# Two fp32 transformer blocks on one core: 64-row band scores issued in pairs, and 16 meta keys padded to 128 rows

## The chip, the core and the metric

The kernel runs on one core of a Trainium2 chip. A core has five engines with a queue each: TensorE (PE; its weight loads are listed apart as PEld), VectorE (DVE), ScalarE (ACT), GpSimd (POOL) and SyncE (SP), which here only issues DMA transfers. TensorE reads SBUF and writes PSUM; VectorE and ScalarE carry results from PSUM to SBUF. The metric is the device time of one execution in microseconds (us), lower is better.

## The reference, cut to what matters

Two blocks run one after the other over 256 tokens of width 2048, all in fp32. The first mixes by a gated scan over eight heads and by an attention over bands of chunks with 16 heads of width 64, then has an MLP of width 8192. The second puts 16 meta tokens in front, has two attentions (A: eight query heads of width 128 on two key heads; B: eight heads, each with two score maps of width 64 and one value of width 128), and keeps only the 256 real tokens. The two attentions that the change touches:

```python
# first block, band attention: 16 heads of width 64
s = jnp.einsum('bhnqd,bhnkd->bhnqk', qc, kb) * (Dh ** -0.5) + bias[:, None]
p = jax.nn.softmax(jnp.where(valid[:, None, :], s, -jnp.inf), axis=-1)
o = jnp.einsum('bhnqk,bhnkd->bhnqd', p, vb)
# second block, mixer A; 272 keys, 16 of them meta tokens
s = jnp.einsum('bkgqd,bksd->bkgqs', qs[0], k) * scale
o = jnp.einsum('bkgqs,bksd->bkgqd', jax.nn.softmax(s, axis=-1), v)
# second block, mixer B
a = jax.nn.softmax(s1, axis=-1) - lam * jax.nn.softmax(s2, axis=-1)
o = jnp.einsum('bhqk,bhkd->bhqd', a, v)
```

## The kernel before, in words

The linear layers are one long stream. `run_stream` (from line 223) walks over all weights in pieces of 1 MB, which SP loads into three buffers (line 240). Each piece is worked in two halves. ScalarE rounds a half to a high part `wh` (line 256, three halves ahead), VectorE makes the low part `wl` (line 268, two halves ahead), and TensorE multiplies both by the operand, which is split in the same way: three fp32r matmuls per tile of 128x128, twelve to a half with 512 columns (line 307), or, in those layers of the second block whose result is wanted transposed, 24 with 272 columns (line 305).

Everything else is a side task, written as a Python generator. `gap` runs at the middle and at the end of a half and advances the tasks of `bg` and `post` by one step, so a task's instructions stand in every engine's queue behind the half in which the step was taken. The order is fixed when the program is built; nothing is scheduled at run time. The queues are in order, and tiles come from pools: ten SBUF tiles `w2`, four PSUM banks `ps`. An instruction that takes a tile over waits until its last reader is done.

`band(c)` (line 544) handles eight heads, and runs twice. In an even step `j` it issues the scores of head `j // 2`: two matmuls over 64 rows (width 64), one of 128 and one of 256 columns (lines 584, 585), with even heads on partitions 0 to 63 and odd heads on 64 to 127; then a fused add and maximum for each (lines 589, 591), a scale and two exponentials (lines 594, 595). In odd steps an earlier head's probabilities are transposed (line 602), copied (line 604), and one step pair later multiplied by the values (lines 613 to 615).

`att_a` (line 925) and `att_b` (line 993) do the second block's mixers, each twice, in eight units of one head and 128 queries. The 272 keys are two blocks of 128 and one of 16 meta keys. `probs_T` transposes the three blocks; the third has 16 columns as weights (line 985). `probs_out` copies them out of PSUM with two instructions (lines 989, 990). The value product adds three matmuls, of which the third has 16 rows (line 970 in A, line 1051 in B). `ev2_nat` (line 809) brings the values into natural order, with those of the meta tokens in a tile of 16 partitions. The scores of B (line 1028) are two matmuls over 64 rows, one on each half of the partitions, issued back to back.

An fp32 matmul (not fp32r) runs as two passes, each a weight load and a matmul in the trace.

Of the kernel before, what the change touches and what calls it, by code (L numbers as in the profile page):

```python
# [27 lines left out]
def two_blocks_kernel(  # L28
# [85 lines left out]
    def split(dst, k0, n, src, scale=None):  # L114
        """dst[:, :, k0:k0+n] <- hi and lo of src [P, n, 256] (times a column per kt)."""
        if scale is None or not isinstance(scale, (list, tuple)):
            hi, lo = dst[:, 0, k0:k0 + n, 0:256], dst[:, 1, k0:k0 + n, 0:256]
            if scale is None:
                act(out=hi, in_=src, func=AF.Copy)
                tt_(out=lo, in0=src, in1=hi.bitcast(F32), op=ALU.subtract)  # L120
            else:
                act(out=hi, in_=src, func=AF.Copy, scale=scale)
                stt(out=lo, in0=src, scalar=scale, in1=hi.bitcast(F32), op0=ALU.mult, op1=ALU.subtract)
            return
        for k in range(n):
            hi, lo = dst[:, 0, k0 + k, 0:256], dst[:, 1, k0 + k, 0:256]
            act(out=hi, in_=src[:, k], func=AF.Copy, scale=scale[k])
            stt(out=lo, in0=src[:, k], scalar=scale[k], in1=hi.bitcast(F32), op0=ALU.mult, op1=ALU.subtract)

    def xpose_split(src, name, g, colscale=None, one=None):  # L130
        """generator: the group g of operand `name` from src [token, 2, 512] natural."""
        dst = op_tile(name, g)
        if name == "z":
            mt = mt_t[0][:, 4 * g:4 * g + 4, :]
            act(out=dst[:, 0, :, 256:NKEY], in_=mt, func=AF.Copy)
            tt_(out=dst[:, 1, :, 256:NKEY], in0=mt, in1=dst[:, 0, :, 256:NKEY].bitcast(F32), op=ALU.subtract)
        for half in range(2):
            p = ps([P, 2, 256])
            for k in range(2):
                for t in range(2):  # L140
                    c = (half * 2 + k) * P
                    nc.tensor.transpose(p[:, k, t * P:(t + 1) * P], src[:, t, c:c + P], ident_)  # L142
            if colscale is not None:
                sc = [colt[:, colscale + 4 * g + 2 * half + k:colscale + 4 * g + 2 * half + k + 1] for k in range(2)]
            else:
                sc = one
            split(dst, 2 * half, 2, p, sc)
            if half == 0:
                yield True
        ops[name, g] = dst  # L150
        yield True

# [53 lines left out]
    class Job:  # L206
        """One block of columns of a layer: 512 with the tokens stationary, or (`keys`) 256 with
        the weights stationary, which leaves the result transposed, the meta tokens behind the others."""
# [125 lines left out]
    def start(issue, prepare):  # L334
# [27 lines left out]
        def rest():  # L362
# [18 lines left out]
            # lower bounds: softmax over the two rows, its first row  # L381
# [162 lines left out]
    def band(c):  # L544
# [29 lines left out]
        for j in range(16 + 4):  # L574
            if j == 5:
                load_bias(1)
            if j % 2 == 0 and j < 16:
                h = j // 2
                pr, e = h // 2, (h % 2) * 64
                if h % 4 == 0:  # L580
                    st[h // 4] = sm([P, 2, 4])
                p = ps([P, 384])
                q0, k0 = qT[e:e + 64, pr], kT[e:e + 64, pr]
                nc.tensor.matmul(p[:, 0:P], lhsT=q0[:, 0:P], rhs=k0[:, 0:P], start=True, stop=True)  # L584
                nc.tensor.matmul(p[:, P:384], lhsT=q0[:, P:256], rhs=k0, start=True, stop=True)  # L585
                s = w2([P, 384])
                mx = sm([P, 4])
                tb = tbs[h // 4][:, h % 4]
                nc.vector.tensor_tensor_reduce(out=s[:, 0:P], in0=p[:, 0:P], in1=tb[:, P:256], scale=1.0, scalar=-3.0e38,
                                               op0=ALU.add, op1=ALU.max, accum_out=mx[:, 0:1])  # L590
                nc.vector.tensor_tensor_reduce(out=s[:, P:384], in0=p[:, P:384], in1=tb, scale=1.0, scalar=-3.0e38,
                                               op0=ALU.add, op1=ALU.max, accum_out=mx[:, 1:2])
                ts_(out=mx[:, 2:4], in0=mx[:, 0:2], scalar1=-1.0, scalar2=None, op0=ALU.mult)
                act(out=s[:, 0:P], in_=s[:, 0:P], func=AF.Exp, bias=mx[:, 2:3], accum_out=st[h // 4][:, 0, h % 4:h % 4 + 1])
                act(out=s[:, P:384], in_=s[:, P:384], func=AF.Exp, bias=mx[:, 3:4], accum_out=st[h // 4][:, 1, h % 4:h % 4 + 1])
                sT[h] = s
# [199 lines left out]
    def ev2_keysT(c, sub):  # L796
        """two heads of transposed keys of the second mixer"""
        def f(accs):
            ensure("rbc")
            if sub == 0:  # L800
                nat["kb", c] = c4([P, 4, NKEY])
            for k in range(2):
                tt_(out=nat["kb", c][:, 2 * sub + k], in0=accs[k], in1=rbc, op=ALU.mult)
            if sub == 1:
                flags.add(("kb", c))
                bg.append(att_b(c))
        return f

    def ev2_nat(key, sub, meta_shape, then=None):
        """256 columns with the tokens back on the partitions, the meta tokens apart"""  # L810
# [6 lines left out]
        def back(t):  # L817
            for _ in range(2):
                yield False
            if sub == 0:  # L820
                nat[key] = c4([P, 2, NCH]), w2(meta_shape)
            v, m = nat[key]
# [13 lines left out]
            act(out=m2[:, cs], in_=p, func=AF.Copy, scale=st2[0:META, 0:1])  # L836
# [7 lines left out]
    def rope(v, nh, qk, t):  # L844
        """v [P, nh, 128] in place, with the gain."""
# [10 lines left out]
    def head_norm(v, nh, dst, parts=P):  # L856
        """dst [parts, nh] <- rsqrt of the mean square of each head of v."""
# [8 lines left out]
    def keys_a():  # L866
# [9 lines left out]
        head_norm(vmA[:, 0], 2, rm, parts=META)  # L876
# [8 lines left out]
        for h in range(2):  # L885
            stt(out=vmA[:, 0, h], in0=vmA[:, 0, h], scalar=rm[:, h:h + 1], in1=qkg[0:META, 1], op0=ALU.mult, op1=ALU.mult)
# [3 lines left out]
        for h in range(2):  # L890
# [3 lines left out]
            nc.tensor.transpose(p[:, 256:NKEY], vmA[:, 0, h], ident[0:META, 0:META])  # L894
# [5 lines left out]
    def transposed(src, dst, scales=None):  # L900
        """dst [P, 4, >=256] <- the four blocks of src, transposed (times a constant each)."""
# [23 lines left out]
    def att_a(c):  # L925
# [18 lines left out]
        for j in range(16 + 4):  # L944
            if j % 2 == 0 and j < 16:
# [8 lines left out]
                s = w2([P, NKEY])  # L954
                act(out=s, in_=p, func=AF.Exp, bias=z[:, 0:1], scale=z[:, 1:2], accum_out=z[:, 2:3])
# [8 lines left out]
            if j % 2 == 1 and 0 <= u < 8:  # L964
# [5 lines left out]
                nc.tensor.matmul(p, lhsT=w[0:META, 2, :], rhs=vmA[:, 1, c], start=False, stop=True)  # L970
# [10 lines left out]

    def probs_T(s, p):
        nc.tensor.transpose(p[:, 0, :], s[:, 0:P], ident_)
        nc.tensor.transpose(p[:, 1, :], s[:, P:256], ident_)
        nc.tensor.transpose(p[0:META, 2, :], s[:, 256:NKEY], ident_)

    def probs_out(p):
        w = w2([P, 3, P])
        nc.vector.tensor_copy(out=w[:, 0:2], in_=p[:, 0:2])
        nc.vector.tensor_copy(out=w[0:META, 2], in_=p[0:META, 2])  # L990
        return w

    def att_b(c):
# [19 lines left out]
        for j in range(16 + 6):  # L1013
            if j % 2 == 1 and 0 <= (j - 3) // 2 < 8:
# [5 lines left out]
                stt(out=e[0], in0=e[1], scalar=z[:, 7:8], in1=e[0], op0=ALU.mult, op1=ALU.add)  # L1020
            if j % 2 == 0 and j < 16:
# [4 lines left out]
                for k in range(2):  # L1026
                    p = ps([P, NKEY])
                    nc.tensor.matmul(p, lhsT=qT[64 * k:64 * k + 64, h, t * P:(t + 1) * P], rhs=kT[64 * k:64 * k + 64, h],  # L1028
                                     start=True, stop=True)
                    s = w2([P, NKEY])  # L1030
                    nc.vector.tensor_tensor_reduce(out=s, in0=p, in1=dist[:, t], scale=1.0, scalar=-3.0e38,
# [3 lines left out]
                for k in range(2):  # L1035
                    act(out=e[k], in_=e[k], func=AF.Exp, bias=z[:, 2 + k:3 + k], scale=slope, accum_out=z[:, 4 + k:5 + k])
# [8 lines left out]
            if j % 2 == 1 and 0 <= u < 8:  # L1045
# [5 lines left out]
                nc.tensor.matmul(p, lhsT=w[0:META, 2, :], rhs=vmB[:, h // 2, h % 2], start=False, stop=True)  # L1051
# [88 lines left out]
    def proj_b(c):  # L1140
# [3 lines left out]
        for u in range(2):  # L1144
            J(w_in_2, 0, 4608 + NCH * c + 256 * u, "z", 4, ev2_nat(("vb", c), u, [META, 2, 2, P]), True)
# [5 lines left out]
    for u in range(2):  # L1151
        J(w_in_2, 0, 1024 + 256 * u, "z", 4, ev2_nat("kv", u, [META, 2, 2, P], lambda: bg.appendleft(keys_a())), True)
# [79 lines left out]
```

## Time and profile before

| | |
|---|---|
| three timed runs | 1972.69 us median (1971.82 to 1972.81) |
| span of the profiled execution | 1971.6 us; the page gives no other time of it, so what lies around the span is read as the median less the span, 1.1 us |
| TensorE matmuls | 1950.7 us busy, 99% |
| TensorE weight loads | 1597.3 us, 81%, beside the matmuls |
| VectorE, ScalarE, GpSimd | 1093.6 us (55%), 900.5 us (46%), 41.7 us (2%) |
| DMA | 344.88 MB, mean 175 GB/s |

A busy share says how long an engine had something in hand, not that it worked at its best. Matmuls are pipelined: the printed duration of one is longer than the time from its start to the next one's, so the cost of a group of matmuls is read from starts. A time in brackets behind a row is how long the engine sat idle before it, with what ended that.

### The profile page before, as it was taken

How to read it: one execution, taken by the hardware profiler on the slowest of the kernel's cores; microseconds unless marked ns; L12 is line 12 of the kernel's file. 1: busy time of each engine (PE TensorE's matmuls, PEld its weight loads, DVE VectorE, ACT ScalarE, POOL GpSimd, SP SyncE). 2: the span in 40 equal slices, each digit the busy share in tenths (PEclk: the TensorE clock that was granted, in tenths of full speed). 3: DMA queues.
4: the chain of work that ended last, by engine and by line, in shares of the span. 5: the costliest groups of instructions: out<-in, count | busy, mean ns of one | idle time of the engine just before them, and what ended most of it. 6: DMA issues, size and time to landing. Idle time of an engine off the chain costs nothing.

```text
span 1971.6 us, 23902 instructions
## 1 busy us (share of the span) xinstructions
PE 1950.7 (99%) x9438; PEld 1597.3 (81%) x9438; DVE 1093.6 (55%) x1555; ACT 900.5 (46%) x1267; POOL 41.7 (2%) x49
## 2 busy tenths in 40 slices
PE   8999999999999999999999999999999999999997
PEld 6888887878888888888888888888888998878886
DVE  5666655544446655554555555446566555566554
ACT  6344344454444445443444344335454444456442
POOL 0000010000000000000000000000000100000000
PEclk9999999999999999999999999999999999999999
DMA  8444464445555556555665555556555533434553
GB/s 307 150 150 169 152 202 142 168 150 169 185 185 184 185 181 191 180 191 184 186 199 183 185 187 171 196 189 211 172 188 175 171 129 129 150 129 150 171 182 117
DMA packets 183441, 344.88 MB, mean 175 GB/s; under 512 B 5840, under 2 KB 28368, under 8 KB 183328
## 3 DMA queue, kind: packets, MB, share of 16 engines
q1 hardware_dynamic: 181632, 337.70, 51.3%
q0 software_dynamic: 1696, 5.65, 0.9%
q8 instruction: 74, 1.21, 0.2%
q14 instruction: 39, 0.32, 0.0%
HBM read 341.23 MB, written 2.10 MB: 174 GB/s over the span
## 4 chain that ended last, share of the span: by engine, by line
PE 92%; issue 6%; DMA 1%; DVE 0%; SPq 0%; POOL 0%; POOLq 0%; DVEq 0%; ACT 0%; ACTq 0%
PE acc L307 78%; PE acc L305 6%; PE sp L142 1%; PE sp L456 1%; DMA raw<-in_w_in_dram 1%; PE sp L1028 1%; PE sp L585 0%; PE sp L949 0%; PE sp L584 0%; PE sp L1051 0%; PE sp L602 0%; PE sp L970 0%; DVE c L1091 0%; PE sp L478 0%; PE sp L1050 0%
## 5 line engine op out<-in xcount | busy, mean ns | idle before, releaser
L268 DVE TENSOR_TENSOR wl<-raw,wh 128x1024 fp32r<-128x1024 f32 (+1 forms) x634 | 770.9, 1218 | 449.8 <-PE acc L307 368.5
L256 ACT ACTIVATE wh<-raw 128x1024 fp32r<-128x1024 f32 (+1 forms) x634 | 667.6, 1055 | 656.3 <-PE acc L307 612.0
L307 PE MATMUL acc<-wh,op_u 128*128 128x512 f32 x1408 | 466.7, 401 | 8.2 <-ACT wh L256 6.7
L307 PE MATMUL acc<-wh,op_v 128*128 128x512 f32 x1024 | 327.0, 395 | 0.0
L307 PE MATMUL acc<-wh,op_h 128*128 128x512 f32 x1024 | 323.9, 394 | 0.0
L307 PEld LDWEIGHTS acc<-wh,op_u 128*128 128x128 f32 x1408 | 265.2, 188 | 71.9 <-ACT wh L256 6.7
L307 PE MATMUL acc<-wl,op_u 128*128 128x512 f32 x704 | 278.3, 395 | 1.0 <-DVE wl L268 1.0
L307 PEld LDWEIGHTS acc<-wh,op_h 128*128 128x128 f32 x1024 | 192.3, 188 | 44.0
L307 PEld LDWEIGHTS acc<-wh,op_v 128*128 128x128 f32 x1024 | 192.3, 188 | 43.5
L307 PE MATMUL acc<-wl,op_h 128*128 128x512 f32 x512 | 201.8, 394 | 0.0
L307 PE MATMUL acc<-wl,op_v 128*128 128x512 f32 x512 | 201.7, 394 | 0.0
L307 PE MATMUL acc<-wh,op_z 128*128 128x512 f32 x512 | 177.4, 407 | 0.0
L307 PEld LDWEIGHTS acc<-wl,op_u 128*128 128x128 f32 x704 | 132.9, 189 | 29.2 <-DVE wl L268 2.2
L305 PE MATMUL acc<-op_z,wh 128*128 128x272 f32 x640 | 130.1, 295 | 0.0
L307 PEld LDWEIGHTS acc<-wh,op_z 128*128 128x128 f32 x512 | 96.1, 188 | 27.6 <-issue 4.3
L307 PEld LDWEIGHTS acc<-wl,op_h 128*128 128x128 f32 x512 | 96.1, 188 | 22.3
L307 PEld LDWEIGHTS acc<-wl,op_v 128*128 128x128 f32 x512 | 96.1, 188 | 21.7
L305 PEld LDWEIGHTS acc<-op_z,wh 128*128 128x128 f32 x640 | 102.4, 188 | 2.5 <-issue 1.1
L307 PE MATMUL acc<-wl,op_z 128*128 128x512 f32 x256 | 100.8, 394 | 0.0
L305 PE MATMUL acc<-op_z,wl 128*128 128x272 f32 x320 | 92.1, 288 | 0.0
L307 PE MATMUL acc<-wh,op_mg 128*128 128x512 f32 x256 | 82.1, 396 | 0.0
L307 PE MATMUL acc<-wh,op_y 128*128 128x512 f32 x256 | 80.6, 394 | 0.0
(262 smaller groups left out, 1664.7 us busy)
## 6 DMA issues: line engine op xcount, KB each, us to landing
raw<-in_w_in_dram SPq DMA_DIRECT2D x138, 1024.0 KB, 4.9
raw<-in_w_up_dram SPq DMA_DIRECT2D x64, 1024.0 KB, 5.4
raw<-in_w_down_dram SPq DMA_DIRECT2D x64, 1024.0 KB, 5.0
raw<-in_w_out_dram SPq DMA_DIRECT2D x32, 1024.0 KB, 5.0
raw<-in_w_branch_a_dram SPq DMA_DIRECT2D x8, 1024.0 KB, 4.9
raw<-in_w_branch_b_dram SPq DMA_DIRECT2D x8, 1024.0 KB, 5.0
raw<-in_w_in_dram SPq DMA_DIRECT2D x4, 512.0 KB, 8.4
res<-in_x_dram SPq DMA_DIRECT2D x4, 512.0 KB, 10.4
```

The lines of the kernel that those rows point to most:

```text
L142: nc.tensor.transpose(p[:, k, t * P:(t + 1) * P], src[:, t, c:c + P], ident_)
L256: act(out=wh[:, k], in_=t[:, k], func=AF.Copy)
L268: tt_(out=wl[:, k], in0=t[:, k], in1=wh[:, k].bitcast(F32), op=ALU.subtract)
L305: nc.tensor.matmul(accs[t], lhsT=b[:, k, sl], rhs=xt[:, a, kk, :], start=st, stop=en)
L307: nc.tensor.matmul(accs[t], lhsT=xt[:, a, kk, sl], rhs=b[:, k, :], start=st, stop=en)
L456: nc.tensor.matmul(p[:, 2 * h + t, :], lhsT=kq[:, h, s], rhs=qp[:, h, s], start=True, stop=True)
L1028: nc.tensor.matmul(p, lhsT=qT[64 * k:64 * k + 64, h, t * P:(t + 1) * P], rhs=kT[64 * k:64 * k + 64, h], start=True, stop=True)
```

## The change

In `band` the even steps that begin a pair of heads (`j % 4 == 0`) now issue the scores of both heads: the 128-column matmul of the one, then of the other, then both 256-column ones, in two PSUM banks; the reduces and exponentials of both heads follow. The odd head's scores thus stand two steps earlier than before.

In the second block the third block of probabilities is 128 wide: a tile comes from `padded`, where GpSimd clears columns 272 to 383, the transpose takes all 128 columns, one copy brings all three blocks out, and the value matmul takes 128 rows. The tiles with the meta tokens' values have 128 partitions and are cleared whole. Comments and docstrings are dropped, so line numbers move.

```diff
-            if j % 2 == 0 and j < 16:
-                h = j // 2
-                pr, e = h // 2, (h % 2) * 64
...
-                p = ps([P, 384])
-                q0, k0 = qT[e:e + 64, pr], kT[e:e + 64, pr]
-                nc.tensor.matmul(p[:, 0:P], lhsT=q0[:, 0:P], rhs=k0[:, 0:P], start=True, stop=True)
-                nc.tensor.matmul(p[:, P:384], lhsT=q0[:, P:256], rhs=k0, start=True, stop=True)
...
+            if j % 4 == 0 and j < 16:
+
+                pr = j // 4
...
+                pair_p = [ps([P, 384]) for _ in range(2)]
+                for b in range(2):
+                    for e in range(2):
+                        q0, k0 = qT[64 * e:64 * e + 64, pr], kT[64 * e:64 * e + 64, pr]
+                        if b == 0:
+                            nc.tensor.matmul(pair_p[e][:, 0:P], lhsT=q0[:, 0:P], rhs=k0[:, 0:P], start=True, stop=True)
+                        else:
+                            nc.tensor.matmul(pair_p[e][:, P:384], lhsT=q0[:, P:256], rhs=k0, start=True, stop=True)
+                for e in range(2):
+                    h, p = 2 * pr + e, pair_p[e]
...
             if sub == 0:
                 nat[key] = c4([P, 2, NCH]), w2(meta_shape)
+                nc.gpsimd.memset(nat[key][1], 0.0)
...
-                s = w2([P, NKEY])
-                act(out=s, in_=p, func=AF.Exp, bias=z[:, 0:1], scale=z[:, 1:2], accum_out=z[:, 2:3])
+                s = padded()
+                act(out=s[:, 0:NKEY], in_=p, func=AF.Exp, bias=z[:, 0:1], scale=z[:, 1:2], accum_out=z[:, 2:3])
...
-                nc.tensor.matmul(p, lhsT=w[0:META, 2, :], rhs=vmA[:, 1, c], start=False, stop=True)
+                nc.tensor.matmul(p, lhsT=w[:, 2, :], rhs=vmA[:, 1, c], start=False, stop=True)
...
+    def padded():
+
+        s = w2([P, 384])
+        nc.gpsimd.memset(s[:, NKEY:384], 0.0)
+        return s
+
...
-        nc.tensor.transpose(p[0:META, 2, :], s[:, 256:NKEY], ident_)
+        nc.tensor.transpose(p[:, 2, :], s[:, 256:384], ident_)
...
-        nc.vector.tensor_copy(out=w[:, 0:2], in_=p[:, 0:2])
-        nc.vector.tensor_copy(out=w[0:META, 2], in_=p[0:META, 2])
+        nc.vector.tensor_copy(out=w, in_=p[:, 0:3])
...
-                nc.tensor.matmul(p, lhsT=w[0:META, 2, :], rhs=vmB[:, h // 2, h % 2], start=False, stop=True)
+                nc.tensor.matmul(p, lhsT=w[:, 2, :], rhs=vmB[:, h // 2, h % 2], start=False, stop=True)
...
-            J(w_in_2, 0, 4608 + NCH * c + 256 * u, "z", 4, ev2_nat(("vb", c), u, [META, 2, 2, P]), True)
+            J(w_in_2, 0, 4608 + NCH * c + 256 * u, "z", 4, ev2_nat(("vb", c), u, [P, 2, 2, P]), True)
```

In `att_b` the first of the two score tiles comes from `padded` in the same way, and its later uses are cut to the first 272 columns.

The queue of TensorE where the first scores of the band stand, before and then after. `sp` are PSUM banks with scores, `c_353` and `c_363` the transposed keys and queries, `acc` the stream's accumulators.

```order
L307 MATMUL acc_2148<-wl_2250,op_u_29_226 128x512
L307 MATMUL acc_2148<-wh_2232,op_u_29_226 128x512
L584 MATMUL sp_2305<-c_353_2136,c_363_2185 128x128
L585 MATMUL sp_2305<-c_353_2136,c_363_2185 128x256
L307 MATMUL acc_2319<-wh_2248,op_u_9_127 128x512
L307 MATMUL acc_2319<-wl_2268,op_u_9_127 128x512
```

```order
L307 MATMUL acc_2148<-wl_2250,op_u_29_226 128x512
L307 MATMUL acc_2148<-wh_2232,op_u_29_226 128x512
L587 MATMUL sp_2305<-c_353_2136,c_363_2185 128x128
L587 MATMUL sp_2306<-c_353_2136,c_363_2185 128x128
L589 MATMUL sp_2305<-c_353_2136,c_363_2185 128x256
L589 MATMUL sp_2306<-c_353_2136,c_363_2185 128x256
L307 MATMUL acc_2329<-wh_2248,op_u_9_127 128x512
```

The second head's two matmuls, which stood two halves of stream further on, now stand among the first head's, in a bank of their own.

The same queue at one unit of mixer A, before and then after. `w` are SBUF tiles with probabilities, `w_1798` the meta tokens' values.

```order
L983 MATMUL sp_11446<-ident,w_1882_11380 128x128
L984 MATMUL sp_11446<-ident,w_1882_11380 128x128
L985 MATMUL sp_11446<-ident,w_1882_11380 16x128
L968 MATMUL sp_11446<-c_1797_10815,w_1888_11404 128x128
L969 MATMUL sp_11446<-c_1797_10815,w_1888_11404 128x128
L970 MATMUL sp_11446<-w_1798_10816,w_1888_11404 128x128
L305 MATMUL acc_11387<-op_z_1700_10140,wh_11321 128x272
```

```order
L997 MATMUL sp_11449<-ident,w_1882_11382 128x128
L998 MATMUL sp_11449<-ident,w_1882_11382 128x128
L999 MATMUL sp_11449<-ident,w_1882_11382 128x128
L976 MATMUL sp_11449<-c_1797_10815,w_1888_11407 128x128
L977 MATMUL sp_11449<-c_1797_10815,w_1888_11407 128x128
L978 MATMUL sp_11449<-w_1798_10816,w_1888_11407 128x128
L305 MATMUL acc_11390<-op_z_1700_10140,wh_11322 128x272
```

Nothing changes place here; the third transpose now writes 128 partitions instead of 16, and the third value matmul reads as many.

The queue of GpSimd at the start of the second block's attention, before and then after.

```order
L719 MEMSET w_1752_10472 128x128
L862 TENSOR_TENSOR sm_11051<-sm_11053,mhalf 128x2
L862 TENSOR_TENSOR sm_11051<-sm_11058,mhalf 128x2
L862 TENSOR_TENSOR sm_11052<-sm_11063,mhalf 16x2
L862 TENSOR_TENSOR sm_11203<-sm_11204,mhalf 128x4
L862 TENSOR_TENSOR sm_11203<-sm_11223,mhalf 128x4
L104 TENSOR_TENSOR sm_11962<-sm_12421,mhalf 128x8
```

```order
L726 MEMSET w_1752_10472 128x128
L829 MEMSET w_1798_10816 128x512
L870 TENSOR_TENSOR sm_11052<-sm_11054,mhalf 128x2
L870 TENSOR_TENSOR sm_11052<-sm_11059,mhalf 128x2
L870 TENSOR_TENSOR sm_11053<-sm_11064,mhalf 16x2
L870 TENSOR_TENSOR sm_11204<-sm_11205,mhalf 128x4
L870 TENSOR_TENSOR sm_11204<-sm_11224,mhalf 128x4
L993 MEMSET w_1874_11351 128x112
L993 MEMSET w_1882_11382 128x112
```

Between the powers (`TENSOR_TENSOR` with `mhalf`, which VectorE waits for) now stand the memsets: 32 of 112 columns, one per unit, and three of 512.

## Rows read from the trace of the kernel before

**Rows 1.** The page: busy time of TensorE, and granted clock in 40 slices.
```profile
PE 1950.7 (99%) x9438; PEld 1597.3 (81%) x9438; DVE 1093.6 (55%) x1555; ACT 900.5 (46%) x1267; POOL 41.7 (2%) x49
PEclk9999999999999999999999999999999999999999
```

**Rows 2.** Waits of TensorE, whole span: waiter, what for, us, times, longest.
```profile
PE acc L307 <- ACT wh L256: 6.7, 1, 6.7
PE acc L307 <- ACT op_u L127: 1.5, 1, 1.5
PE acc L307 <- DVE wl L268: 1.0, 1, 1.0
```

**Rows 3.** A stretch of stream alone: length, busy (x) per engine, clock, DMA, GB/s.
```profile
865.00:973.00 108.00, 108.00 (x470) 87.56 (x468) 54.84 (x50) 43.16 (x42) 0.53 (x1) 1.00 0.57 186
```

**Rows 4.** Timeline of TensorE at the band's first head: start, duration, line, tiles.
```profile
298.21 0.40 PE L307 MATMUL acc<-wh,op_u 128*128 128x512 f32 x1
298.54 0.49 PE L584 MATMUL sp<-c,c 64*128 64x128 f32 x2
298.87 0.59 PE L585 MATMUL sp<-c,c 64*128 64x256 f32 x2
299.39 0.50 PE L307 MATMUL acc<-wh,op_u 128*128 128x512 f32 x1
299.73 0.40 PE L307 MATMUL acc<-wl,op_u 128*128 128x512 f32 x1
```

**Rows 5.** Timeline of TensorE at one unit of mixer A.
```profile
1597.03 0.27 PE L984 MATMUL sp<-ident,w 128*128 128x128 f32 x1
1597.14 0.27 PE L985 MATMUL sp<-ident,w 128*16 128x128 f32 x1
1597.25 0.39 PE L968 MATMUL sp<-c,w 128*128 128x128 f32 x2
1597.47 0.39 PE L969 MATMUL sp<-c,w 128*128 128x128 f32 x2
1597.79 0.48 PE L970 MATMUL sp<-w,w 16*128 16x128 f32 x2
1598.43 0.29 PE L305 MATMUL acc<-op_z,wl 128*128 128x272 f32 x1
```

**Rows 6.** Timeline of TensorE at the first scores of mixer B.
```profile
1646.75 0.29 PE L305 MATMUL acc<-op_z,wh 128*128 128x272 f32 x1
1646.97 0.73 PE L1028 MATMUL sp<-c,c 64*128 64x272 f32 x4
1647.63 0.39 PE L305 MATMUL acc<-op_z,wh 128*128 128x272 f32 x1
1647.86 0.29 PE L305 MATMUL acc<-op_z,wl 128*128 128x272 f32 x1
```

**Rows 7.** Groups of TensorE by line and form: count, busy us, mean ns.
```profile
L584 PE MATMUL sp<-c,c 64*128 64x128 f32 x32 | 7.8, 322 | 0.0
L970 PE MATMUL sp<-w,w 16*128 16x128 f32 x32 | 7.7, 321 | 0.0
L1051 PE MATMUL sp<-w,w 16*128 16x128 f32 x32 | 7.7, 321 | 0.0
```

**Rows 8.** Groups of GpSimd by line and form.
```profile
L104 POOL TENSOR_TENSOR sm<-sm,mhalf 128x4 f32<-128x4 f32 x4 | 7.6, 1897 | 203.6 <-DVE sm L103 201.3 <-ACT wh L256 2.3
L550 POOL MEMSET c<- 64x256 f32 x4 | 1.2, 306 | 19.1 <-DMA c<-in_relb_dram 19.1
L719 POOL MEMSET w<- 128x128 f32 x1 | 0.2, 218 | 0.0
```

**Rows 9.** Line 983 from 1596 to 1603: durations, first and last start.
```profile
L983 PE MATMUL sp<-ident,w x2: 270/271/272, 1596.9 to 1601.8; 128*128 128x128 f32 x2
```

**Rows 10.** Timeline of VectorE behind the band's first scores.
```profile
299.60 0.29 DVE L589 CUSTOM_DVE_ANT_0 w<-sp,c 128x128 f32<-128x128 f32 x1 [0.20 <-PE sp L585]
300.36 1.22 DVE L268 TENSOR_TENSOR wl<-raw,wh 128x1024 fp32r<-128x1024 f32 x1
```

More of the change, by code (lines that the diff above doesn't have):

```diff
@@ L576, in band @@
                 load_bias(1)
-            if j % 2 == 0 and j < 16:
-                h = j // 2
-                pr, e = h // 2, (h % 2) * 64
-                if h % 4 == 0:
-                    st[h // 4] = sm([P, 2, 4])
-                p = ps([P, 384])
-                q0, k0 = qT[e:e + 64, pr], kT[e:e + 64, pr]
-                nc.tensor.matmul(p[:, 0:P], lhsT=q0[:, 0:P], rhs=k0[:, 0:P], start=True, stop=True)
-                nc.tensor.matmul(p[:, P:384], lhsT=q0[:, P:256], rhs=k0, start=True, stop=True)
[L586 to L596, printed above, removed]
@@ new lines, in band @@
+            if j % 4 == 0 and j < 16:
+                pr = j // 4
+                if pr % 2 == 0:
+                    st[pr // 2] = sm([P, 2, 4])
+                pair_p = [ps([P, 384]) for _ in range(2)]
[9 more added lines that the diff above has]
+                    s = w2([P, 384])
+                    mx = sm([P, 4])
+                    tb = tbs[h // 4][:, h % 4]
+                    nc.vector.tensor_tensor_reduce(out=s[:, 0:P], in0=p[:, 0:P], in1=tb[:, P:256], scale=1.0,
+                                                   scalar=-3.0e38, op0=ALU.add, op1=ALU.max, accum_out=mx[:, 0:1])
+                    nc.vector.tensor_tensor_reduce(out=s[:, P:384], in0=p[:, P:384], in1=tb, scale=1.0,
+                                                   scalar=-3.0e38, op0=ALU.add, op1=ALU.max, accum_out=mx[:, 1:2])
+                    ts_(out=mx[:, 2:4], in0=mx[:, 0:2], scalar1=-1.0, scalar2=None, op0=ALU.mult)
+                    for b, (c0, c1) in enumerate(((0, P), (P, 384))):
+                        act(out=s[:, c0:c1], in_=s[:, c0:c1], func=AF.Exp, bias=mx[:, 2 + b:3 + b],
+                            accum_out=st[h // 4][:, b, h % 4:h % 4 + 1])
+                    sT[h] = s
@@ L835, in back @@
                 nc.tensor.transpose(p[:, k * P:(k + 1) * P], t[:, k, 256:NKEY], ident_)
-            act(out=m2[:, cs], in_=p, func=AF.Copy, scale=st2[0:META, 0:1])
+            act(out=m2[0:META, cs], in_=p, func=AF.Copy, scale=st2[0:META, 0:1])
             if sub == 1:
@@ L875, in keys_a @@
             head_norm(kv[:, t, 0:256].rearrange("p (h d) -> p h d", d=P), 2, rk[:, t])
-        head_norm(vmA[:, 0], 2, rm, parts=META)
+        head_norm(vmA[0:META, 0], 2, rm, parts=META)
         yield True
@@ L885, in keys_a @@
         for h in range(2):
-            stt(out=vmA[:, 0, h], in0=vmA[:, 0, h], scalar=rm[:, h:h + 1], in1=qkg[0:META, 1], op0=ALU.mult, op1=ALU.mult)
+            stt(out=vmA[0:META, 0, h], in0=vmA[0:META, 0, h], scalar=rm[:, h:h + 1], in1=qkg[0:META, 1], op0=ALU.mult, op1=ALU.mult)
         yield True
@@ L893, in keys_a @@
                 nc.tensor.transpose(p[:, t * P:(t + 1) * P], kv[:, t, h * P:(h + 1) * P], ident_)
-            nc.tensor.transpose(p[:, 256:NKEY], vmA[:, 0, h], ident[0:META, 0:META])
+            nc.tensor.transpose(p[:, 256:NKEY], vmA[0:META, 0, h], ident[0:META, 0:META])
             nc.scalar.copy(out=kT[:, h], in_=p)
@@ L980, in att_a @@
             ropet.clear()
+    def padded():
+        s = w2([P, 384])
+        nc.gpsimd.memset(s[:, NKEY:384], 0.0)
+        return s
     def probs_T(s, p):
@@ L1019, in att_b @@
                 ts_(out=z[:, 7:8], in0=z[:, 7:8], scalar1=z[:, 4:5], scalar2=st2[:, 1:2], op0=ALU.mult, op1=ALU.mult)
-                stt(out=e[0], in0=e[1], scalar=z[:, 7:8], in1=e[0], op0=ALU.mult, op1=ALU.add)
+                stt(out=e[0][:, 0:NKEY], in0=e[1], scalar=z[:, 7:8], in1=e[0][:, 0:NKEY], op0=ALU.mult, op1=ALU.add)
             if j % 2 == 0 and j < 16:
@@ L1027, in att_b @@
                     p = ps([P, NKEY])
+                    if k == 0:
+                        s = padded()
+                    else:
+                        s = w2([P, NKEY])
                     nc.tensor.matmul(p, lhsT=qT[64 * k:64 * k + 64, h, t * P:(t + 1) * P], rhs=kT[64 * k:64 * k + 64, h],
                                      start=True, stop=True)
-                    s = w2([P, NKEY])
-                    nc.vector.tensor_tensor_reduce(out=s, in0=p, in1=dist[:, t], scale=1.0, scalar=-3.0e38,
+                    nc.vector.tensor_tensor_reduce(out=s[:, 0:NKEY], in0=p, in1=dist[:, t], scale=1.0, scalar=-3.0e38,
                                                    op0=ALU.add, op1=ALU.max, accum_out=z[:, k:k + 1])
@@ L1035, in att_b @@
                 for k in range(2):
-                    act(out=e[k], in_=e[k], func=AF.Exp, bias=z[:, 2 + k:3 + k], scale=slope, accum_out=z[:, 4 + k:5 + k])
+                    act(out=e[k][:, 0:NKEY], in_=e[k][:, 0:NKEY], func=AF.Exp, bias=z[:, 2 + k:3 + k], scale=slope, accum_out=z[:, 4 + k:5 + k])
                 eT[i], st[i] = e, z
@@ L1151, in two_blocks_kernel @@
     for u in range(2):
-        J(w_in_2, 0, 1024 + 256 * u, "z", 4, ev2_nat("kv", u, [META, 2, 2, P], lambda: bg.appendleft(keys_a())), True)
+        J(w_in_2, 0, 1024 + 256 * u, "z", 4, ev2_nat("kv", u, [P, 2, 2, P], lambda: bg.appendleft(keys_a())), True)
     proj_b(0)
```

## The prediction

> **What bounds the kernel now.** I read the page's busy shares first, then the waits, then single stretches of the timeline. TensorE is busy 99% of the span, at the full granted clock (2.4 GHz) in all 40 slices [rows 1]. The list of waits gives TensorE three waits, 9.2 us together, all for the first weights and operands of the program [rows 2]; from then on no engine and no transfer is ever late for it. VectorE (55%), ScalarE (46%) and GpSimd (2%) run beside it, and their idle time is no cost. So the forecast is a count of TensorE time: what this engine no longer does comes off the end, unless a wait that was hidden comes up.
>
> One unit is needed. In a stretch of pure weight stream 470 matmuls, 468 of them of 512 columns, fill 108.00 us: 0.23 us each [rows 3]. A matmul of 272 columns in the same stream is then 0.12 us. Both are times from start to start; the durations printed beside a matmul overlap and must not be added.
>
> **Band scores, before.** For one head the timeline shows a stream matmul at 298.21, the two 64-row score matmuls (two passes each) at 298.54 and 298.87, the stream again at 299.39 and 299.73 [rows 4]. From 298.21 to 299.73 are 1.52 us, of which two stream matmuls explain 0.46; the head costs 1.06. How much of that is work? An fp32 pass of 128 columns is 0.11 us (two passes from 1597.25 to 1597.47 [rows 5]), one of 256 columns 0.22 by its columns. Two of each make 0.66. The other 0.40 us lie at the two ends: the first 64-row pass starts 0.33 after the last stream matmul instead of 0.23, the first stream matmul comes late after the last pass, and the one behind it 0.34 later instead of 0.23, since it had no weights loaded ahead. I call this the toll of changing the number of rows and coming back.
>
> **Two row halves side by side.** The trace already has such pairs: in the second mixer of the second block, two 64-row matmuls of 272 columns, one in each half of the rows, two passes each. From 1646.75 to 1647.86 are 1.11 us [rows 6]; less two stream matmuls of 0.12 that is 0.87. One pass of 272 columns is 0.23 by its columns. Four passes in turn plus the toll would be 0.92 + 0.40 = 1.32; two steps of two passes side by side plus one toll are 0.46 + 0.40 = 0.86. The row says side by side, and one toll for both.
>
> So a pair of heads after the change costs between 0.40 + 0.66 = 1.06 (side by side) and 0.40 + 1.32 = 1.72 (in turn). I take 1.06, by the row of the same kind. There are 16 heads (32 passes of each form [rows 7]), so 8 pairs: 16 x 1.06 = 17.0 before, 8 x 1.06 = 8.5 after, **8.5 us less**; at the other bound 17.0 - 13.8 = 3.2 less.
>
> **Meta keys padded, TensorE.** The value matmul over 16 rows starts 0.32 after its neighbour's start, where that neighbour is 0.22 of work, and the second stream matmul behind it stands at 1598.43. From 1597.47 to 1598.43 are 0.96; less 0.22 for L969 and 0.12 for one stream matmul it costs 0.62. Its two passes are 0.22 of work, as those of L969 with 128 rows; the rest, 0.40, is the same toll [rows 5]. With 128 rows there is no change of rows: 0.22. Two lines with 32 passes each are 32 matmuls [rows 7]: 32 x 0.40 = **12.8 us less**. The third transpose loads 128 columns as weights instead of 16. The one before it, with 128, and it itself both take 0.11 to the next start [rows 5], so I add nothing; were the load to show fully as one more pass it would be 32 x 0.11 = 3.5 us.
>
> **The other engines.** GpSimd gets 32 memsets of 128x112 and three of 128x512. One of 128x128 takes 0.218 us, one of 64x256 0.306 [rows 8]; 32 x 0.2 are 7 us on an engine that is 2% busy, and the large ones lie between 0.2 and 0.9 us each. They hide because a probability tile is cleared when it is handed out, and its transposes come three steps later: two transposes of consecutive tiles, two steps apart, start at 1596.9 and 1601.8 [rows 9], so the cover is 4.9 x 3/2 = 7.3 us. What can be queued ahead of a memset on GpSimd is a power of 1.9 us [rows 8], or a DMA issue; what is queued behind one is the next power, which VectorE wants, and further memsets. Instructions of VectorE and ScalarE that write the same tile now also wait for the memset, but that one waits for the readers for which they had to wait anyway. The copy of the transposed probabilities becomes one instead of two: less VectorE time, off the path.
>
> In the band the odd head's scores move two steps forward, and with them everything they issue: two more fused reduces and a scale on VectorE, two exponentials on ScalarE, behind which stand the splits of the weights. On VectorE one head takes from 299.60 to 300.36, 0.76 us, and the next weight split ends 1.22 later, at 301.58; it is wanted by the third half ahead, two halves of twelve matmuls (2 x 2.8 us) after 299.39, at about 304.9 [rows 10]. A second head's 0.76 uses part of a margin of 3.3 us. It also puts the weight load that the split releases on SP's queue 0.76 later; the pure stream gets 186 GB/s with no wait [rows 3], and the band's stretch wants less.
>
> **Sum.** 12.8 + 8.5 = 21.3 us. The profiled execution's span is 1971.6, so 1950.3 after. The median of the three runs, 1972.69, is 1.1 above that span; with the same surround the time is **1951.4 us**. Differences under 0.2% (3.9 us) are about what cannot be told from no change.
>
> **Rivals.**
> 1. *The passes keep their order.* If starts on TensorE must follow the program, the second pass of head one must start before the first of head two; of eight passes (four of 0.11, four of 0.22) only neighbours of different heads overlap, and a pair takes 2 x 0.11 + 3 x 0.22 = 0.88 of work instead of 0.66: 8 x 0.22 = 1.8 less gain, 1953.2 us. Against it: by that order the pair in [rows 6] would be 3 x 0.23 + 0.40 = 1.09, and it is 0.87. Chance 8%.
> The Trainium skill, "TensorE: Matmul & The Clock Gate", Part 3, The mechanism, states that order: matmuls start and end strictly in program order, and only weight loads are pulled ahead. By it the sum would be rival 1's; the row above is closer to free halves.
> 2. *No overlap in the band*, only half the tolls: 3.2 instead of 8.5, 1956.7 us. For it: four matmuls per pair instead of two, with two PSUM banks taken at once. Against: the same rows. 6%.
> 3. *The change does not do what it says for the padded rows:* the gap around the 16-row matmul comes from its wait on VectorE's copy and stays. Then only the band's 8.5 is won: 1964.2 us. Against it: the delay of the stream behind it, which waits for nothing of that kind. 4%.
> 4. *VectorE's burst uncovers.* If the pair's double burst made a weight split late by 0.5 to 1 us at each of 8 pairs, 4 to 8 us come back: 1955 to 1959. It decides only beyond the 3.3 us of margin. 5%.
> 5. *Slower:* the memsets are late and TensorE stands at the third transpose. It loses more than it gains by 0.2% from (21.3 + 3.9) / 32 = 0.79 us per tile, that is when a memset ends 7.3 + 0.8 = 8.1 us after its tile was handed out; at 1 us each the time is 1951.4 + 32 = 1983.4. For it: GpSimd is one queue in order, and the tiles come from a pool of ten that is in use. Against: the longest instruction there is 1.9 us, and nothing in the program stands between a free tile and its memset. 3%.
>
> **Chances.** My forecast 74%, rivals 8, 6, 4, 5 and 3%. Faster than by 0.2%: forecast and rivals 1 to 4, less a little for a stall between 4 and 5: 0.95; within 0.2%: 0.02; slower: 0.03. The range runs from 1949.5 (forecast, less the 1.0 us by which the three runs differ and 0.02 us of rounding at each of 40 tolls) to 1957.5 (past rivals 1 and 2, half of 4, and the 3.5 us of the third transpose).
>
> **What would show it.** Right: eight blocks of 64-row scores in the band, each moving the stream by 1.06 us, with two matmuls starting within a few hundredths; the third transpose, value matmuls and stream at 0.11 steps with no hole; 35 more memsets; TensorE's waits still only the three at the start. Wrong: pairs of 1.3 or 1.7 us (rivals 1, 2), holes left at the value matmul (3), waits of the stream for VectorE in the band (4), waits of the transposes for GpSimd (5).

## The result, and the profile after

The changed kernel takes 1952.10 us (median of four runs, 1951.59 to 1952.61); the kernel before, on the same chip, 1972.59 (1971.82 to 1972.81). The ratio is 0.9896, with an interval of 0.9882 to 0.9910: 20.5 us less. The span of the profiled execution is 1950.3 us, 21.3 below the 1971.6 of before.

The page of the kernel after, busy time of the engines and granted clock, answers [rows 1]:

```profile
PE 1930.4 (99%) x9438; PEld 1590.4 (82%) x9438; DVE 1091.9 (56%) x1523; ACT 899.4 (46%) x1267; POOL 48.6 (2%) x84
...
PEclk9999999999999999999999999999999999999999
```

TensorE executes the same 9438 matmuls as before, at the same clock, and is busy 20.3 us less (1950.7 to 1930.4). So no matmul was removed. The lost time stands in the profile as busy time, because the printed duration of a late matmul covers its delay: time with no matmul in hand fell only from 20.9 to 19.9 us. VectorE has 32 instructions fewer (the copies of transposed probabilities, one instead of two), GpSimd 35 more (the memsets) and 6.9 us more time.

TensorE's waits in the kernel after, columns as in [rows 2]:

```profile
PE acc L307 <- ACT wh L256: 6.3, 1, 6.3
PE acc L307 <- DVE wl L268: 1.0, 1, 1.0
PE acc L307 <- ACT op_u L127: 0.8, 1, 0.8
```

These are still the three waits at the start of the program and no others. They make 8.1 us instead of 9.2, and in two other executions of the same kernel 8.5 and 8.6; that start is not the change's doing.

The band's first pair of heads, timeline of TensorE in the kernel after, answers [rows 4]:

```profile
297.33 0.40 PE L307 MATMUL acc<-wh,op_u 128*128 128x512 f32 x1
297.65 0.49 PE L587 MATMUL sp<-c,c 64*128 64x128 f32 x4
297.98 0.60 PE L589 MATMUL sp<-c,c 64*128 64x256 f32 x4
298.51 0.50 PE L307 MATMUL acc<-wh,op_u 128*128 128x512 f32 x1
298.85 0.40 PE L307 MATMUL acc<-wl,op_u 128*128 128x512 f32 x1
```

Counted from the first row, the starts are those of [rows 4] to within 0.02 us, with x4 where x2 stood. From 297.33 to 298.85 are 1.52; less two stream matmuls of 0.23 the pair costs 1.06, as one head did. The second head adds nothing.

One unit of mixer A in the kernel after, timeline of TensorE, answers [rows 5]:

```profile
1592.30 0.27 PE L998 MATMUL sp<-ident,w 128*128 128x128 f32 x1
1592.41 0.27 PE L999 MATMUL sp<-ident,w 128*128 128x128 f32 x1
1592.52 0.39 PE L976 MATMUL sp<-c,w 128*128 128x128 f32 x2
1592.74 0.39 PE L977 MATMUL sp<-c,w 128*128 128x128 f32 x2
1592.97 0.39 PE L978 MATMUL sp<-w,w 128*128 128x128 f32 x2
1593.11 0.37 PE L305 MATMUL acc<-op_z,wh 128*128 128x272 f32 x1
1593.32 0.29 PE L305 MATMUL acc<-op_z,wl 128*128 128x272 f32 x1
```

L978 starts 0.23 after L977 instead of 0.32, and from L977 to the second stream matmul are 0.58 us where there were 0.96. Less 0.22 for L977 and 0.12 for one stream matmul, the value matmul costs 0.24 instead of 0.62 (over all 32, by the starts of their neighbours, 0.228 instead of 0.614). The third transpose, L999, is followed after 0.11, as the second is: its 128 columns of weights instead of 16 cost nothing.

### The profile page after: what moved, and what is told of

Its sections match the earlier page's. It is cut to its first block, busy times and chain, and to the rows that moved or that the text cites. A ratio compares the mean times of both kernels' runs of the same rounds, so it can differ in the third digit from the quotient of the medians.

```text
span 1950.3 us, 23923 instructions
## 1 busy us (share of the span) xinstructions
PE 1930.4 (99%) x9438; PEld 1590.4 (82%) x9438; DVE 1091.9 (56%) x1523; ACT 899.4 (46%) x1267; POOL 48.6 (2%) x84
## 4 chain that ended last, share of the span: by engine, by line
PE 91%; issue 7%; DVE 1%; DMA 0%; ACT 0%; SPq 0%; POOL 0%; POOLq 0%; DVEq 0%; ACTq 0%
PE acc L307 78%; PE acc L305 6%; PE sp L142 1%; PE sp L456 1%; PE sp L1045 1%; DMA raw<-in_w_in_dram 0%; PE sp L957 0%; PE sp L609 0%; DVE c L1107 0%; PE sp L478 0%; DVE wl L268 0%; PE sp L1066 0%; PE sp L621 0%; PE sp L1067 0%; PE sp L1065 0%
```

## The experiments

All compare with the kernel before on the same chip. "Block" is the time by which a group of matmuls delays the stream, read as above, from start to start. The theory was the prediction's: a *toll* of 0.40 us whenever TensorE leaves 128 rows and comes back, and free overlap of the two row halves.

**Each part alone.** The first is the kernel before with only the new band, the second the kernel after with the old band:

```
 e1  if j % 4 == 0 and j < 16:      # kernel before + pairs of heads (the diff's band part)
 e2  if j % 2 == 0 and j < 16:      # kernel after, band as before
```

> The kernel before with the band's change alone: both heads of a pair issue their 64-row scores side by side, the 16 meta keys stay as they were. My theory is a toll of 0.40 us at each block of matmuls over other than 128 rows, and two row halves that work at the same time: a band block costs 1.06 us for two heads instead of 1.06 for one, 8 blocks fewer, 8.3 to 8.5 us less, so about 1964.2 us; the value matmuls over 16 rows still cost 0.62 each. Rival, the gain is all from the padding (the band is hidden or neutral): 1972.6 us, the same as before. Rival, the passes keep program order: 6.6 us less, 1966.0 us, a block of 1.28.

> The changed kernel with the band put back to one head at a time; the meta keys stay padded to 128 rows. My theory: 32 value matmuls cost 0.22 to 0.23 us instead of 0.61 to 0.62, 12.3 to 12.8 us less, so about 1960.2 us, and together with the band alone the two parts add up to the whole change (20.5 us). Rival, the hole at the 16-row matmul is its wait for VectorE's copy: nothing gained, 1972.6 us. Rival, GpSimd's memsets cost time that the band's gain hides in the whole change: above 1961 us, with waits of the transposes for GpSimd.

The band alone takes 1963.79 us (ratio 0.9954, 0.9939 to 0.9969) against 1972.72: 8.9 less. The padding alone takes 1960.22 (0.9936, 0.9921 to 0.9951): 12.5 less. Together 21.4, the whole 20.5; each median is uncertain by half a microsecond or so. In the first the block of a pair is 1.054 us and the value matmul still 0.614; in the second the value matmul is 0.228. Within the uncertainty of the medians the two parts add up.

**Order of the passes.** Rival 1 held that passes start in program order. This kernel issues both matmuls of one head before those of the other:

```
-                for b in range(2):
-                    for e in range(2):
+                for e in range(2):
+                    for b in range(2):
```

> The changed kernel with the band's four matmuls in another order: first both of the one head, then both of the other, still in one block and on the two row halves. If each half of the rows has its own queue and starts whatever is next for it, the order does not matter: a block of 1.06 us and 1952.1 us. If starts keep the program's order (rival 1 of the prediction), the second head's first pass can only start beside the first head's last: work of 0.66 + 0.66 - 0.22 = 1.10, a block of 1.50 us, 8 x 0.44 = 3.5 us more, 1955.6 us. A look-ahead of limited depth would lie between.

It takes 1952.25 us (0.9895, 0.9878 to 0.9911), as the kernel after, and the block is 1.061. Timeline of TensorE in this kernel, the first pair:

```profile
298.08 0.40 PE L307 MATMUL acc<-wh,op_u 128*128 128x512 f32 x1
298.41 0.50 PE L587 MATMUL sp<-c,c 64*128 64x128 f32 x4
298.73 0.61 PE L589 MATMUL sp<-c,c 64*128 64x256 f32 x4
299.27 0.50 PE L307 MATMUL acc<-wh,op_u 128*128 128x512 f32 x1
299.61 0.40 PE L307 MATMUL acc<-wl,op_u 128*128 128x512 f32 x1
```

And what the trace says of its two lines in the same stretch (durations in ns; first and last start; form):

```profile
L587 PE MATMUL sp<-c,c x4: 272/322/373, 298.4 to 298.6; 64*128 64x128 f32 x4
...
L589 PE MATMUL sp<-c,c x4: 376/377/378, 298.7 to 299.0; 64*128 64x256 f32 x4
```

The program's order is 128 columns of head one (L587, two passes), 256 columns of head one (L589, two passes), then the same of head two. The trace has all four passes of L587 before the first of L589. So head two's first matmul overtook head one's second: each row half ran through its own matmuls, although up to three passes of the other half stood ahead of them in the queue. With starts in program order the block would have been 0.66 + 0.40 plus 0.44 for head two's 256-column passes, which would have nothing left to lie beside: 1.50 us, which the measured 1.061 excludes. Rival 1 falls, and "the queues are in order", in the words on the kernel before, does not hold for matmuls on different row halves. The Trainium skill, "TensorE: Matmul & The Clock Gate", Part 3, The mechanism, states that matmuls start and end strictly in program order. For matmuls on different row halves this trace disagrees.

**Is it the two halves?** Here both heads of a pair read rows 0 to 63:

```
-                        q0, k0 = qT[64 * e:64 * e + 64, pr], kT[64 * e:64 * e + 64, pr]
+                        q0, k0 = qT[0:64, pr], kT[0:64, pr]
```

> The changed kernel with both heads of a pair on the same half of the rows: the odd heads take the queries and keys of the even one, so the odd heads' scores are not those of the reference; everything else is as in the changed kernel. The number of blocks and of tolls stays, and only the work side by side is gone. My theory: a block is 0.40 + 4 x 0.11 + 4 x 0.22 = 1.72 us, 8 x 0.66 = 5.3 us more, 1957.4 us. Rival, the gain was only the halved number of tolls: a block of 1.06 and 1952.1 us. Rival, with no overlap the toll comes once per head: 2.1 us and 1960.6 us, no gain left.

1957.66 us (0.9925, 0.9910 to 0.9940), block 1.706. Timeline of TensorE in this kernel, the first pair:

```profile
298.04 0.40 PE L307 MATMUL acc<-wh,op_u 128*128 128x512 f32 x1
298.37 0.71 PE L587 MATMUL sp<-c,c 64*128 64x128 f32 x4
298.92 1.03 PE L589 MATMUL sp<-c,c 64*128 64x256 f32 x4
299.87 0.50 PE L307 MATMUL acc<-wh,op_u 128*128 128x512 f32 x1
300.21 0.39 PE L307 MATMUL acc<-wl,op_u 128*128 128x512 f32 x1
```

The groups last 0.71 and 1.03 instead of 0.50 and 0.61: on one half the passes run in turn. This is rival 2's price, to 0.02 us. Of the 8.3 us that the 8 pairs win in the trace, 8 x (1.706 - 1.055) = 5.2 come from the overlap, and the rest from 8 tolls instead of 16.

**Rows or wait?** Rival 3 said that the hole at the value matmul was its wait for VectorE's copy. Here the padded tile, the memsets and the single copy stay, but the matmul reads 64 of its rows:

```
-  nc.tensor.matmul(p, lhsT=w[:, 2, :], rhs=vmA[:, 1, c], start=False, stop=True)
+  nc.tensor.matmul(p, lhsT=w[0:64, 2, :], rhs=vmA[0:64, 1, c], start=False, stop=True)   # and in B
```

> The changed kernel with the value matmul of the meta keys over 64 rows instead of 128 (memsets, transposes and the copy as in the changed kernel). If the toll is for leaving 128 rows, whatever the number is, it comes back at all 32: 0.61 instead of 0.23 us each, 12.3 us more, about 1964.4 us. Rival, the hole belonged to a very short matmul (16 rows) or to the two separate copies: 0.23 us each and 1952.1 us.

1964.85 us (0.9958, 0.9944 to 0.9973): 12.6 us slower than the order test, which ran on the same chip, and which differs from the kernel after by nothing that the time shows. The value matmul is back at 0.616. Its group of TensorE by line and form in this kernel (count, busy us, mean ns):

```profile
L978 PE MATMUL sp<-w,w 64*128 64x128 f32 x32 | 7.8, 322 | 0.0
```

And the same group in the kernel after:

```profile
L978 PE MATMUL sp<-w,w 128*128 128x128 f32 x32 | 6.2, 275 | 0.0
```

With 64 rows it lasts 322 ns, as with 16 (321 [rows 7]); with 128 it lasts 275. So the toll comes with 16 rows and with 64 alike; other numbers were not tried. In the kernel before, the weight loads (`LDWEIGHTS`) of 31 of the 32 value matmuls named a semaphore that VectorE raises; here none of the 64 loads names one, and the toll is the same. Rival 3 falls.

What the toll consists of can be read from the weight loads. One unit of this kernel, timeline of the weight loads and then of the matmuls:

```profile
1598.23 0.30 PEld L977 LDWEIGHTS sp<-c,w 128*128 128x128 f32 x2
1598.65 0.29 PEld L978 LDWEIGHTS sp<-w,w 64*128 64x128 f32 x2
1599.07 0.19 PEld L305 LDWEIGHTS acc<-op_z,wh 128*128 128x128 f32 x1
```

```profile
1598.34 0.39 PE L977 MATMUL sp<-c,w 128*128 128x128 f32 x2
1598.65 0.49 PE L978 MATMUL sp<-w,w 64*128 64x128 f32 x2
1599.07 0.40 PE L305 MATMUL acc<-op_z,wh 128*128 128x272 f32 x1
```

L977 keeps 128 rows, and its weights start to load 0.11 us before it. Those of L978, and those of the stream behind it, start to load only with their matmul. In the kernel before this is so, to 0.003 us, at all 67 changes from 128 rows to fewer and at all 67 changes back; of the 9173 other matmuls over 128 rows whose load could be paired, 24 show it, and the median load starts 0.23 us ahead. At the unit of [rows 5] each of the two changes makes its first matmul and the one behind it about 0.1 us late: 0.09 + 0.10 + 0.09 + 0.11 is the toll. Why TensorE does not load ahead across the change stays open.

**How much cover have the memsets?** Each 128x112 memset is issued eight times:

```
-        nc.gpsimd.memset(s[:, NKEY:384], 0.0)
+        for _ in range(8):
+            nc.gpsimd.memset(s[:, NKEY:384], 0.0)
```

> The changed kernel with each of the 32 memsets of 128x112 issued eight times: GpSimd does 224 more of 0.19 us, 42.6 us of work. If the memsets are covered by the steps between a tile's handing out and its transposes (7.3 us, of which eight take 1.5), nothing moves: 1952.1 us and no wait of TensorE for GpSimd. If they are near the path (rival 5 of the prediction), up to 1.3 us come at each of 32 tiles: up to 1994 us.

1952.06 us (0.9897, 0.9882 to 0.9912), beside 1952.38 for the kernel after, run again on that chip. GpSimd by line and form in this kernel:

```profile
L994 POOL MEMSET w<- 128x112 f32 x256 | 49.0, 194 | 135.9 <-DVE w L1034 75.9 <-PE sp L978 22.8 <-PE sp L1000 19.8
```

And in the kernel after:

```profile
L993 POOL MEMSET w<- 128x112 f32 x32 | 5.6, 190 | 172.3 <-DVE w L1033 92.1 <-PE sp L999 36.6 <-PE sp L978 35.1
L829 POOL MEMSET w<- 128x512 f32 x3 | 1.6, 532 | 4.3 <-PE sp L978 4.3
```

One memset is 0.19 us and eight are 1.55, 43 us more on GpSimd, and TensorE waits for none of it. Rival 5 is excluded at eight times the price. Paired in order, each memset of the kernel after ends at least 14.8 us before the first transpose of its tile, twice the 7.3 us of cover that the prediction reckoned with; how long a memset would show was not tried.

The repeat of the kernel after served as a base:

> The changed kernel unchanged, on the same chip as the three that follow, as their base: 1952.1 us, a band block of 1.05 to 1.06 us, a value matmul of 0.23.

It gave 1952.38 us (0.9898, 0.9883 to 0.9912), with a band block of 1.055, a value matmul of 0.228 and a block of mixer B of 0.858.

**Fewer tolls still.** If a toll is paid per block, two blocks joined save one. Mixer B has 16 blocks of four passes of 272 columns; this kernel scores both query halves of a head in one block, in four PSUM banks:

```
-            if j % 2 == 0 and j < 16:
+            if j % 4 == 0 and j < 16:
+                pp = [[ps([P, NKEY]) for _ in range(2)] for _ in range(2)]
+                for t in range(2):
+                    for k in range(2):
+                        nc.tensor.matmul(pp[t][k], ...)      # then the softmax of both halves
```

> A further step by the same theory: in mixer B of the second block the scores of both query halves of a head are issued in one block (four 64-row matmuls, four PSUM banks at once) instead of two blocks of two. Work stays at eight passes two by two, 4 x 0.23 = 0.92, with one toll of 0.40: 1.32 us instead of 2 x 0.86, 8 x 0.40 = 3.2 us less than the changed kernel, 1948.9 us. Rival, all four banks at once make TensorE wait for the readers of the block before, or the ten SBUF tiles run short: waits of the scores for VectorE or ScalarE, and 1952 us or more.

1950.36 us (0.9890, 0.9873 to 0.9906): 2.0 below the kernel after on the same chip (1952.38), where 3.2 were expected. Six of the eight blocks cost 1.316 to 1.326, as expected; the other two 1.76 and 2.61. Timeline of TensorE at the second of those two, the block of 2.61:

```profile
1734.35 0.40 PE L307 MATMUL acc<-wh,op_z 128*128 128x512 f32 x1
1734.67 1.18 PE L1040 MATMUL sp<-c,c 64*128 64x272 f32 x6
1736.43 0.72 PE L1040 MATMUL sp<-c,c 64*128 64x272 f32 x2 [0.58 <-ACT junk L1072]
1737.08 0.50 PE L307 MATMUL acc<-wh,op_z 128*128 128x512 f32 x1
```

The fourth matmul waits for a PSUM bank. ScalarE's part of the same stretch:

```profile
1735.66 0.37 ACT L1071 ACTIVATE c<-sp,sm 128x128 f32<-128x128 f32 x1 [3.36 <-DVE w L1003]
1735.93 0.36 ACT L1072 ACTIVATE junk<-sp,sm 128x128 bf16<-128x128 f32 x1
```

ScalarE scales and squares an older value product out of that bank (L1071, L1072), and does so late: by the bracket it had waited for VectorE's copy of the probabilities (L1003). At the block of 1.76 the fourth matmul also starts just after that square, at 1651.02 us. The last kernel lets the bank go earlier: VectorE takes the product out, ScalarE squares the copy in SBUF, and the combination of the two maps on VectorE moves behind it:

```
-                act(out=o[:, t, hs], in_=p, func=AF.Copy, scale=ri[:, u:u + 1])
-                act(out=junk[:, 0:P], in_=p, func=AF.Square, scale=ri[:, u:u + 1], accum_out=ss[:, u:u + 1])
+                ts_(out=o[:, t, hs], in0=p, scalar1=ri[:, u:u + 1], scalar2=None, op0=ALU.mult)
+                act(out=junk[:, 0:P], in_=o[:, t, hs], func=AF.Square, accum_out=ss[:, u:u + 1])
```

> Two query halves in one block, as in the run before it, where six of eight blocks cost the expected 1.32 us and two cost 1.76 and 2.61, waiting for the bank that ScalarE's square still read. Here VectorE takes the value product out of its bank right after the copy, ScalarE squares the SBUF copy, and the difference of the two maps (reciprocal to scalar_tensor_tensor) stands behind both in VectorE's queue. My theory: all eight blocks at 1.32 us, 8 x 0.40 = 3.2 us less than the changed kernel, 1949.2 us against 1952.4. Rival, VectorE's longer queue gives the wait back somewhere else: blocks still over 1.32 or waits of the stream for VectorE, and about 1950.4 us as before.

> The changed kernel unchanged, as the base of the run beside it: 1952.1 to 1952.4 us.

It takes 1949.31 us (1949.04 to 1949.85; ratio to before 0.9883, 0.9865 to 0.9901), and the kernel after on the same chip 1952.29 (1952.15 to 1952.76; 0.9899, 0.9881 to 0.9917): 3.0 us less. The intervals of the two ratios overlap, but the single runs do not. Timeline of TensorE in this kernel, at the block that had waited:

```profile
1734.91 0.40 PE L307 MATMUL acc<-wh,op_z 128*128 128x512 f32 x1
1735.24 1.19 PE L1033 MATMUL sp<-c,c 64*128 64x272 f32 x8
1736.36 0.51 PE L307 MATMUL acc<-wh,op_z 128*128 128x512 f32 x1
1736.70 0.39 PE L307 MATMUL acc<-wl,op_z 128*128 128x512 f32 x1
```

Eight passes in one group, no wait: 1.79 us from the first row to the last, less 0.46 is 1.33; over all eight blocks 1.315 to 1.326. Four steps of 0.23 and one toll of 0.40 make 1.32. So it is faster than the kernel after by a little less than the 3.2 expected. Against the kernel with the wait (1950.36) it is 1.05 lower, but those two were not timed side by side. The earlier release and the moved combination were changed together, so which of them ended the wait was not separated.

## Why the prediction was right, step by step

- *TensorE is the bound, and what it no longer does comes off the end.* Shown by the two parts alone, which each gave their own term, and by the list of waits, which got no new line.
- *A pair of heads costs what one head did.* Predicted 1.06, and 8 x 1.06 = 8.5 us less. Over all blocks: 16 of 1.048 before, 16.8 us; 8 of 1.055 after, 8.4 us; 8.3 less. The single-part run gave 8.9. The mechanism is separated by one half for both (1.706) and by the order (1.061).
- *The value matmul loses the toll.* Predicted 32 x 0.40 = 12.8. By all 32: 0.614 to 0.228, 0.386 each, 12.3 less; the single-part run gave 12.5. The toll was 0.014 us too large, read from rows with two decimals; over 32 that is 0.45 us.
- *The third transpose costs nothing.* 0.11 to its neighbour, with the upper bound of 3.5 us unused.
- *The memsets hide.* Predicted about 0.2 us each and 0.2 to 0.9 for the large ones; measured 0.19 and 0.53, and eight times as many hide too. The cover was underrated (7.3 us against 14.8 and more), on the safe side.
- *VectorE's double burst stays inside its margin.* It grew as foreseen. VectorE in the kernel after, behind the first pair:

```profile
298.71 0.29 DVE L595 CUSTOM_DVE_ANT_0 w<-sp,c 128x128 f32<-128x128 f32 x1 [0.20 <-PE sp L589]
...
299.47 0.28 DVE L595 CUSTOM_DVE_ANT_0 w<-sp,c 128x128 f32<-128x128 f32 x1
...
300.22 1.22 DVE L268 TENSOR_TENSOR wl<-raw,wh 128x1024 fp32r<-128x1024 f32 x1
302.44 1.23 DVE L268 TENSOR_TENSOR wl<-raw,wh 128x1024 fp32r<-128x1024 f32 x1 [1.00 <-ACT wh L256]
```

  From 298.71 to 300.22 are 1.51 us for two heads, where one took 0.76 [rows 10]. The split ends at 301.44; by the prediction's rule it is wanted 5.6 us after 298.51, at 304.1. So 2.7 us of margin are left. Splits and matmuls paired in order, the trace has the first use at 304.41, 3.0 us after the split; in the kernel before it was at 306.33, a margin of 4.7 where the prediction read 3.3. The engine itself stands idle for 1.00 us before the next split. How large a burst would uncover the split was not tried.
- *The sum.* Counted block by block, 8.3 + 12.3 = 20.6 us of the span's 21.3 are the change. The other 0.7 can be the start, whose three waits are 1.1 us shorter in this execution and vary from run to run; it was not isolated. The predicted span, 1950.3, was met to the decimal with a sum 0.7 too large, so in part by that luck.
- *What lies around the span.* The prediction took the median less the span, 1.1 us, from different executions. In the runs after, where time and span of one execution are both known, it is 1952.06 - 1950.3 = 1.8. That is the 0.7 by which the measured median stands above the predicted 1951.4.
- *The range.* Its lower end is 1951.4 - 1.0 - 40 x 0.02 = 1949.6, not 1949.5; nothing hangs on it.

## What to carry to other kernels

Where TensorE is the bound, look at the starts around every matmul that uses fewer than 128 rows: the stream loses 0.39 to 0.40 us per excursion here, for two passes as for eight, so pad a lone one to 128 rows with zeros, and gather those that must stay narrow into one block that uses both row halves. How long the block can be is set by the PSUM banks, so check who reads them last. Read costs from start to start and count blocks over the whole trace, because durations of overlapped matmuls don't add up.

## What was not expected of the hardware

- A matmul on the other row half overtook three passes that stood ahead of it in the queue: in the order test all four passes of L587 start from 298.4 to 298.6, before the first of L589 at 298.7. The two orders tried take the same time (1952.25 against 1952.10 us).
- The toll is the same for a matmul of 16 rows (0.614 us), of 64 rows (0.616), and, to 0.01 us, for a block of eight passes (1.32 for 0.92 of work). It goes with weights that are not loaded ahead, at all 134 changes of the row count in the kernel before.
